# Order of the first stage of a transformer layer: projection weights, context tokens and the planner's price for 32-row products

## The chip, the cores and the metric

The kernel runs on one core of one Trainium2 chip. The metric is the device time of one execution in microseconds (us), given as the median of several runs. One execution has also been taken by the hardware profiler; all rows below come from that execution. A core has a matrix engine (TensorE, PE in the rows; its weight loads are PEld), a vector engine (DVE), a scalar engine (ACT), a general engine (GpSimd, POOL in the rows) and a queue engine that issues the transfers (SyncE, SP).

## The reference

The reference is one layer on 512 tokens of width 1024, with 256 context tokens beside them. Cut to what matters here:

```python
mod_lat = (silu(c) @ w_ada + b_ada); mod_ctx = (silu(c_ctx) @ w_ada + b_ada)
sa, sca, ga, sf, scf, gf = split(mod_lat, 6); csa, csca, ... = split(mod_ctx, 6)
h_lat = rmsnorm(x, attn_norm_w) * (1 + sca) + sa          # 512 x 1024
h_ctx = rmsnorm(ctx, attn_norm_w) * (1 + csca) + csa      # 256 x 1024
proj  = h @ w_in            # q, k, v of 4 differential heads, and low-rank q, kv of 4 MLA heads
...                         # rotary turn of q and k (latent tokens only), attention over 768 keys
x = x + ga * (mix @ w_out)
x = x + gf * moe(rmsnorm(x, ffn_norm_w) * (1 + scf) + sf) # 32 experts, top 4 of each token
out = rmsnorm(x, final_norm_w)
```

## The kernel before

The program first records every operation with its operands, and a **planner** (class `Plan`) then puts them in order. Each operation has a level; an engine takes, of the operations that could start first in the planner's own clock, the one with the lowest level. The planner's clock comes from `Plan.cost` (a duration for each operation) and from a model of the transfers as one bus. The order found is fixed: on the chip each engine runs its list in that order and waits where an operand is not there yet. Every recorded operation therefore has the same line, L282, in the profile, and is told apart by its tiles. Memory is planned as well: a tile can be placed only when an older tile of its ring has been used up, and, for names that are not in the `free` list of a store, only in the order of recording. A store can follow another one in the same memory: `att` and what stands on it (`rot`, with the rotary tables `trig` and the scratch tiles `rope1`, `rope2`) can be opened only when every operation on the store `start` has been placed and done. `start` holds the tokens `xt`, the modulation weights `wa`, and the scratch tiles `hv`.

The first stage goes like this:

- `load_wa(j)` brings the modulation weights of block j (2 MB, four transfers). Blocks 0, 2, 1 and 3 are loaded in this order, into 12 buffers for 16 transfers, so that block 3 waits for buffers of block 0.
- `modulation(j)` makes eight products of 32 rows (`sc<-wa,silp` in the rows), copies the sum out on ACT (`mrow<-sc`), brings it into columns with four small products (`oo<-pick,mrow`), and finishes `mod` and `gsc` on DVE. The tile `pa` that these small products write has the name `oo`.
- `normed` takes the root mean square of the tokens (squares on ACT, twelve tiny operations `rs_*` on DVE, then `xt<-xt,rs_y`).
- `modulated(k, which, ...)` turns 128 columns of the normed tokens (transposes `pj<-K,xt` and `tr<-K,xt`), applies scale and shift on ACT (`hv`), and splits the result into a high and a low part, `hTh` on DVE and `hTl` on DVE for the latent tokens (which = 0), on POOL for the context tokens (which = 1). The eight k of the latent tokens come in two groups of four; the second group needs block 3.
- `weights(src, n)` loads a chunk of projection weights in four transfers (`craw`, two buffers) and splits each into eight pairs `cwh` (ACT) and `cwl` (DVE).
- The projection loop takes chunk after chunk. The first chunk gives q and k of head 0: four tiles of 128 tokens, each with 8 x 3 products (`mm3`), in two banks named `pj` and two named `sc`. Each bank is read out by `rope`, which needs `trig` and writes on DVE and POOL (`rot`). Then come a product for the context tokens (`pj<-hTh,cwh`) and the next chunk, v, which wants the same four banks.
- Beside this, at level 3, run 64 transfers of further modulation weights (also shown as `wa`), scaled on ACT and summed on POOL (`ac<-ac,wa`).

After that the kernel has attention, output projection, routing, and 32 experts whose weights (`raw`, 12 MB each) are streamed.

Of the kernel before, what the change touches and what calls it, by code (L numbers as in the profile page):

```python
# [14 lines left out]
PSUM = bass.MemoryType.PSUM  # L15
DRAM = bass.MemoryType.DRAM

P = 128
NT = 4
# [181 lines left out]
class Plan:  # L201
# [22 lines left out]
    def cost(self, op, args):  # L224
        def cols(ap):
            n = 1
            for d in ap.shape[1:]:
                n *= d
            return n
        n = cols(args[0])  # L230
        if op.eng == "PE":
            if op.name == "transpose":
                return 0.107
            if args[2].dtype == F32:
                return 4 * max(n, 128) / 2400 / (2 if args[0].shape[0] == SMALL else 1)
            return max(n, 240) / 2400 * PEF / (2 if args[0].shape[0] == SMALL else 1)
        if op.eng == "ACT":
            extra = 0.1 if "accum_out" in op.kw or "bias" in op.kw else 0.0
            return 0.08 + extra + cols(args[1]) / 1200
        if op.eng == "POOL":  # L240
            return 0.06 + n / (1000 if op.name == "memset" else 247 if op.name.startswith(("tensor_scalar", "scalar_"))
                               else 420)
        n = max([cols(a) for a in args[:3] if hasattr(a, "shape")])
        fast = (op.name in ("tensor_copy", "tensor_scalar", "memset")
                and all(b.store.name not in ("ps", "mps") for b in op.bases))
        return 0.07 + n / (1850 if fast else 960)
# [85 lines left out]
def body(ctx, tc, x, ctxt, cc, w_ada, colw, b_arow, w_qk, w_v, w_m, w_uq, w_ukv, lams, w_out, ffn_w, router_w,  # L332
# [12 lines left out]
    const = store("const")  # L345
    small = store("small", const, free=("rs_m", "rs_i", "rs_y", "rs_t"))
    dram = store("dram", space=DRAM)
    ps = store("ps", free=("pj", "tr", "sc"), space=PSUM)
    start = store("start", small)
    att = store("att", small, (start,))  # L350
    rpl = store("rot", att)
# [128 lines left out]

    def modulated(k, which, t0, n):
        dst = slice(t0 * P, (t0 + n) * P)
        pt = bank(*(("pj", 2), ("pj", 2), ("tr", 1))[turn[0] % 3])
        turn[0] += 1
        for t in range(n):
            T.transpose(pt[:, t * P:(t + 1) * P], xt[t0 + t][:, k * P:(k + 1) * P], ident)
        hv = start.tile([P, n * P], F32, name="hv", bufs=3, padded_shape=[P, 512])
        S.activation(hv, pt[:, :n * P], AF.Identity, scale=gsc[:, k, which:which + 1], bias=mod[:, k, which:which + 1])
        V.tensor_copy(hTh[k][:, dst], hv)
        return (V if which == 0 else G).tensor_tensor(hTl[k][:, dst], hv, hTh[k][:, dst].bitcast(F32), op=OP.subtract)  # L490
# [20 lines left out]
    for k in range(4):  # L511
        modulated(k, 0, 0, NT)
    modulation(1)
    modulated_by = modulation(3)
    for k in range(4, KT):
        modulated(k, 0, 0, NT)


    plan.level = 4
# [2 lines left out]
    chunks = [qk_in[0], v_in[0], qk_in[1], qk_in[2], v_in[1], qk_in[3], (w_m[:, :, 0:256], 256, "cq", 0),  # L522
              (w_m[:, :, 256:448], 192, "ckv", 0)]

    def weights(src, n):
        for g in range(4):
            raw = pj.tile([P, 2, n], F32, name="craw", bufs=CRAW, padded_shape=[P, 2, 256])
            SP.dma_start(raw, src[:, 2 * g:2 * g + 2, :])
            for k in range(2):
                plan.side = 2.5  # L530
                a = pj.tile([P, n], F32R, name="cwh", bufs=CW, padded_shape=[P, 256])
                b = pj.tile([P, n], F32R, name="cwl", bufs=CW, padded_shape=[P, 256])
                split(raw[:, k, :], a, b)
                plan.side = EVAC
                yield a, b

    first = list(weights(*chunks[0][:2]))
    plan.level, plan.side = 0, None
    plan.level = 2.6
    for t in range(NCT):  # L540
        SP.dma_start(xt[NT + t], ctxt[t * P:(t + 1) * P, :])
    plan.level = 0
    normed(NT, NCT)
    for k in range(KT):
        ctx_ready = modulated(k, 1, NT, NCT)
# [42 lines left out]
    for ci, (src, n, kind, arg) in enumerate(chunks):  # L588
        cw = first if ci == 0 else list(weights(src, n))
        if kind == "v":  # L590
            heads["v", arg] = [att.tile([P, NKT, 256], F32R, name=n, bufs=2) for n in ("dvh", "dvl")]
        rot = []
        for t in range(NT if kind in ("cq", "qk") else NKT):
            ts = slice(t * P, (t + 1) * P)
            o = bank(*(("sc", 2) if ci < 2 and t % 2 else ("pj", 2)))
            for k, (a, b) in enumerate(cw):
                mm3(o[:, :n], hTh[k][:, ts], hTl[k][:, ts], a, b, k == 0, k == KT - 1,
                    **({"after": (modulated_by,)} if k == 0 else {}))
            if kind == "qk":
                rot.append(rpl.tile([P, 256], F32, name="rot", bufs=ROT))  # L600
                rope(o[:, 0:256], 4, t, rot[t])
            elif kind == "v":
                split(o[:, 0:256], *[v[:, t, :] for v in heads["v", arg]])
            elif kind == "cq":
                cq.append(rpl.tile([P, 256], F32, name="rot", bufs=ROT))
                S.copy(cq[t], o[:, 0:256])
                mj = rpl.tile([P, 256], F32, name="rope1", bufs=1)
                S.activation(mj, cq[t], AF.Square, scale=0.0625, accum_out=mss[:, 2 * t:2 * t + 1])
            else:
                ckv.append(rpl.tile([P, 192], F32, name="rot", bufs=ROT, padded_shape=[P, 256]))  # L610
                S.copy(ckv[t], o[:, 0:192])
                if t < NT:
                    rope(ckv[t][:, 128:192], 1, t, kr[:, t * 64:(t + 1) * 64])
                else:
                    G.tensor_copy(kr[:, t * 64:(t + 1) * 64], ckv[t][:, 128:192])
                mk = rpl.tile([P, P], F32, name="rope2", bufs=1, padded_shape=[P, 256])
                S.activation(mk, ckv[t][:, 0:128], AF.Square, scale=128.0 ** -0.5,
                             accum_out=mss[:, 2 * t + 1:2 * t + 2])
        if kind == "qk":
            kt = bank("pj", 2)  # L620
            for k, (a, b) in enumerate(cw):
                mm3(kt[:, :NCT * P], a[:, P:], b[:, P:], hTh[k][:, NT * P:], hTl[k][:, NT * P:], k == 0, k == KT - 1,
                    **({"after": (ctx_ready,)} if k == 0 else {}))
            A, B = ([att.tile([P, w], F32R, name=f"{name}{c}", bufs=2) for c in range(2)]
                    for name, w in (("dqs", NT * P), ("dks", KEYS)))
            Cl = att.tile([P, KEYS], F32R, name="dkl", bufs=2)
            qt = side_by_side([r[:, :P] for r in rot], A)
            for c, r in enumerate((LOW, HIGH)):
                stack_q(qt, r, DIFF_SCALE, A[c])
            main = side_by_side([r[:, P:] for r in rot], B + [Cl])  # L630
            for pt, d in ((main, slice(0, NT * P)), (kt, slice(NT * P, KEYS))):
                for c, r in enumerate((LOW, HIGH)):
                    stack_k(pt, r, d, B[c], Cl)
            heads[arg] = (A, B, Cl)
# [945 lines left out]
```

## Time and profile before

| what | us |
|---|---|
| median of 3 runs | 1553.77 |
| lowest and highest of them | 1551.37 and 1563.34 |
| the profiled execution, its own time | 1554.69 |
| its span, from the first to the last instruction | 1552.9 |

The span is what the rows cover; the profiled execution's own time is 1.8 us longer, and it lies 0.92 us above the median. TensorE was busy 1426.8 us of the span, DVE 975.9, ACT 820.8, POOL 627.2. A timeline row gives the start, the length, the engine, the operation with its tiles (written <- read), and in brackets how long the engine had been idle and what it waited for.

### The profile page before, as it was taken

To read this page: it belongs to the slowest core of one execution; us is meant where nothing else is said; L and a number is where in the kernel's file an instruction comes from. 1 tells how busy PE (TensorE), PEld (TensorE's weight loads), DVE (VectorE), ACT (ScalarE), POOL (GpSimd) and SP (SyncE) were. 2 spreads that over 40 slices of the span, in tenths; PEclk is the share of its full clock that TensorE was granted. 3 is DMA by queue.
4 is the path that set the end of the run, shared out by engine and by line. 5 is a ranking of instruction groups with operands and counts; after the bars stand their busy time and mean duration, and the time that the engine had idled before them with its cause. 6 is when DMAs were issued, how large, how long until landed. Compare 5 with 4: busy or idle time off the path is not lost.

```text
span 1552.9 us, 21067 instructions
## 1 busy us (share of the span) xinstructions
PE 1426.8 (92%) x7251; PEld 938.9 (60%) x7251; DVE 975.9 (63%) x1387; ACT 820.8 (53%) x1200; POOL 627.2 (40%) x544
## 2 busy tenths in 40 slices
PE   5798998998869999999999999999999999999993
PEld 2787887887646565464554646446364554636772
DVE  3878876776768666384563836547274562736995
ACT  3668866674537555263452635436263452635872
POOL 0553342002465354562735626364462734423111
PEclk9899999998969999999999999999999999999996
DMA  9433333007777999999999999999999999999944
GB/s 348 132 116 114 98 109 136 1 28 250 274 260 267 354 397 391 402 404 393 396 404 389 393 388 395 400 392 396 402 392 398 392 399 397 389 391 396 417 175 138
DMA packets 90895, 478.00 MB, mean 308 GB/s; under 512 B 12309, under 2 KB 14997, under 8 KB 42144
## 3 DMA queue, kind: packets, MB, share of 16 engines
q1 hardware_dynamic: 83040, 459.82, 75.9%
q0 software_dynamic: 7744, 16.79, 4.7%
q8 instruction: 58, 0.95, 0.2%
q14 instruction: 53, 0.43, 0.1%
HBM read 465.40 MB, written 18.24 MB: 311 GB/s over the span
## 4 chain that ended last, share of the span: by engine, by line
DMA 35%; PE 12%; issue 3%; DVE 2%; ACT 0%; SPq 0%; POOL 0%; DVEq 0%; POOLq 0%; ACTq 0%
DMA raw<-in_w 34%; PE gy L282 4%; PE gg L282 4%; PE gu L282 4%; DMA acc_d<-ys,si 1%; DVE wl L282 0%; PE tr L282 0%; DMA raw<-acc_d 0%; DVE raw L282 0%; ACT wh L282 0%; DVE fs L282 0%; ACT xh L282 0%; DVE act L282 0%; DVE rs_t L282 0%; POOL acc_d L1103 0%
## 5 line engine op out<-in xcount | busy, mean ns | idle before, releaser
L282 DVE TENSOR_TENSOR wl<-raw,wh 128x1024 fp32r<-128x1024 f32 x432 | 509.1, 1227 | 53.0 <-ACT wh L282 38.9
L282 ACT CAST wh<-raw 128x1024 fp32r<-128x1024 f32 x432 | 436.4, 1051 | 95.8 <-DMA raw<-in_w 31.1
L1103 POOL DMA_INDIRECT acc_d<-ys,si x17 | 123.2, 7245 | 219.4 <-DVE ys L282 219.4
L282 DVE TENSOR_SCALAR act<-gu 112x1024 f32<-112x1024 f32 (+1 forms) x32 | 31.7, 991 | 278.8 <-PE gu L282 278.8
L282 PE MATMUL gg<-raw,xh 128*64 128x512 f32 x448 | 163.0, 602 | 13.6 <-DMA raw<-in_w 13.6
L282 POOL TENSOR_SCALAR g<-g 112x1024 f32<-112x1024 f32 (+1 forms) x32 | 71.2, 2225 | 251.0 <-ACT g L282 251.0
L282 PE MATMUL gu<-raw,xh 128*64 128x512 f32 x448 | 160.9, 594 | 0.0
L282 ACT COPY g<-gg 112x1024 f32<-112x1024 f32 (+1 forms) x32 | 26.4, 825 | 248.4 <-PE gg L282 248.4
L282 POOL TENSOR_TENSOR ac<-ac,wa 128x512 f32<-128x512 f32 x56 | 77.0, 1376 | 123.8 <-ACT wa L282 110.7
L282 POOL TENSOR_SCALAR krhc<-K,krh 128x64 bf16<-128x64 f32 (+1 forms) x116 | 117.2, 1020 | 6.3 <-PE tr L282 6.3
L282 PE MATMUL gy<-raw,ah 128*64 128x512 f32 x448 | 116.7, 598 | 0.0
L282 PE MATMUL gg<-wh,xh 128*112 128x512 f32 x304 | 105.0, 407 | 2.6 <-ACT wh L282 1.5
L282 PE MATMUL gg<-wh,xl 128*112 128x512 f32 x304 | 99.9, 398 | 0.2 <-DVE xl L282 0.2
L282 PE MATMUL gg<-wl,xh 128*112 128x512 f32 x304 | 97.3, 397 | 1.1 <-DVE woraw L282 0.9
L282 PE MATMUL gy<-wh,ah 128*112 128x512 f32 x272 | 87.0, 400 | 12.1 <-ACT wh L282 12.1
L282 PE MATMUL gu<-wh,xl 128*112 128x512 f32 x288 | 95.1, 399 | 0.0
L282 PE MATMUL gu<-wh,xh 128*112 128x512 f32 x288 | 93.1, 396 | 0.0
L282 PE MATMUL gu<-wl,xh 128*112 128x512 f32 x288 | 92.1, 400 | 0.0
L282 PEld LDWEIGHTS gg<-raw,xh 128*64 128x64 f32 x448 | 42.9, 136 | 80.7 <-DMA raw<-in_w 41.6
L282 PE MATMUL gy<-wl,ah 128*112 128x512 f32 x272 | 88.0, 404 | 2.2
L282 PEld LDWEIGHTS gu<-raw,xh 128*64 128x64 f32 x448 | 47.5, 137 | 63.3 <-issue 62.6
L282 PE MATMUL gy<-wh,al 128*112 128x512 f32 x272 | 85.0, 394 | 0.0
(409 smaller groups left out, 2921.1 us busy)
## 6 DMA issues: line engine op xcount, KB each, us to landing
raw<-in_w SPq DMA_DIRECT2D x380, 1024.0 KB, 21.9
wa<-in_w_ada SPq DMA_DIRECT2D x64, 256.0 KB, 3.1
wa<-in_w_ada SPq DMA_DIRECT2D x16, 512.0 KB, 10.1
craw<-in_w_qk SPq DMA_DIRECT2D x16, 256.0 KB, 3.3
woraw<-in_w_out SPq DMA_DIRECT2D x8, 512.0 KB
raw<-in_w SPq DMA_DIRECT2D x8, 512.0 KB, 10.6
xt<-in_x SPq DMA_DIRECT2D x4, 512.0 KB
craw<-in_w_v SPq DMA_DIRECT2D x8, 256.0 KB, 3.7
```

Of the source, the lines that this page charges most:

```text
L282: getattr(self.engines[op.eng], op.name)(*args, **kw)
L1103: nc.gpsimd.indirect_dma_start(dst, bass.IndirectOffsetOnAxis(ap=si, axis=0), ys, None, bounds_check=halves * NT * P - 1, oob_is_err=False ...
```

## The change

Five edits, all in what the planner is given:

1. `Plan.cost` prices a product that writes 32 rows at a quarter instead of in full (64 rows stay at half).
2. The transfers and splits of the first chunk's weights get levels 0.1 and 0.2 (before: the first transfer 4, the splits 2.5; the later three transfers of the chunk keep 0.5).
3. The norm and `modulated` of the context tokens get level 0.3 instead of 0. The transfers of the context tokens keep 2.6.
4. `modulated` of the context tokens writes the one bank `oo` instead of the three `pj` and `tr`, and `oo` joins the `free` list.
5. The first product of each projection waits for the last transpose of the latent tokens (before: for the last product of modulation block 3), and for a tile of context tokens on the last `hTl` of the context tokens.

```diff
@@ class Plan, cost
             if args[2].dtype == F32:
-                return 4 * max(n, 128) / 2400 / (2 if args[0].shape[0] == SMALL else 1)
-            return max(n, 240) / 2400 * PEF / (2 if args[0].shape[0] == SMALL else 1)
+                return 4 * max(n, 128) / 2400 / {32: 4, 64: 2}.get(args[0].shape[0], 1)
+            return max(n, 240) / 2400 * PEF / {32: 4, 64: 2}.get(args[0].shape[0], 1)
@@ body
-    ps = store("ps", free=("pj", "tr", "sc"), space=PSUM)
+    ps = store("ps", free=("pj", "tr", "sc", "oo"), space=PSUM)
@@ modulated
-        pt = bank(*(("pj", 2), ("pj", 2), ("tr", 1))[turn[0] % 3])
+        pt = bank(*((("pj", 2), ("pj", 2), ("tr", 1)), (("oo", 1),))[which][turn[0] % (1 if which else 3)])
         turn[0] += 1
         for t in range(n):
-            T.transpose(pt[:, t * P:(t + 1) * P], xt[t0 + t][:, k * P:(k + 1) * P], ident)
+            modulated.moved = T.transpose(pt[:, t * P:(t + 1) * P], xt[t0 + t][:, k * P:(k + 1) * P], ident)
@@ after the second group of modulated
-    modulated_by = modulation(3)
+    modulation(3)
     for k in range(4, KT):
         modulated(k, 0, 0, NT)
+    modulated_by = modulated.moved
@@ weights
-    def weights(src, n):
+    def weights(src, n, low=2.5):
...
-                plan.side = 2.5
+                plan.side = low
...
-    first = list(weights(*chunks[0][:2]))
+    plan.level, plan.side = 0.1, 0.1
+    first = list(weights(*chunks[0][:2], 0.2))
     plan.level, plan.side = 0, None
     plan.level = 2.6
     for t in range(NCT):
         SP.dma_start(xt[NT + t], ctxt[t * P:(t + 1) * P, :])
-    plan.level = 0
+    plan.level = 0.3
     normed(NT, NCT)
@@ the projection loop
-                    **({"after": (modulated_by,)} if k == 0 else {}))
+                    **({"after": (modulated_by,) if t < NT else (ctx_ready,)} if k == 0 else {}))
```

## Rows read from the trace of the kernel before

**Rows 1.** The profile page: shares of the chain that ended last, by engine.

```profile
DMA 35%; PE 12%; issue 3%; DVE 2%; ACT 0%; SPq 0%; POOL 0%; DVEq 0%; POOLq 0%; ACTq 0%
```

**Rows 2.** Busy time by stretch (us: length, engines, PE clock, DMA share, GB/s).

```profile
0.00:47.20 47.20, 25.56 (x126) 11.22 (x126) 20.62 (x60) 18.74 (x33) 6.96 (x10) 0.84 0.83 305
...
80.00:360.00 280.00, 261.62 (x1878) 235.69 (x1879) 213.00 (x446) 204.37 (x411) 78.81 (x68) 0.97 0.28 88
...
828.00:1384.00 556.00, 532.58 (x2414) 290.98 (x2413) 291.75 (x277) 243.66 (x293) 258.62 (x205) 1.00 1.01 395
```

**Rows 3.** Timeline of the transfer queue SP, 10 to 36 us.

```profile
10.20 12.74 SPq L282 DMA_DIRECT2D wa<-in_w_ada  x12
...
34.09 2.95 SPq L282 DMA_DIRECT2D craw<-in_w_qk  x2
```

**Rows 4.** Timeline of PE, 32 to 57 us.

```profile
32.83 1.05 PE L282 MATMUL sc<-wa,silp 128*32 128x512 f32 x4 [0.23 <-DMA wa<-in_w_ada]
...
42.38 1.86 PE L282 MATMUL oo<-pick,mrow 128*128 128x2 f32 x8 [7.15 <-ACT mrow L282]
...
47.18 0.58 PE L282 MATMUL sc<-cwl,hTh 128*128 128x256 f32 x1 [2.40 <-DVE cwl L282]
...
55.81 0.44 PE L282 MATMUL pj<-K,xt 128*128 128x128 f32 x2 [0.53 <-ACT hv L282]
```

**Rows 5.** Timeline of ACT, 29 to 50 us.

```profile
29.64 0.59 ACT L282 COPY mrow<-sc 128x512 f32<-128x512 f32 x1 [0.52 <-PE sc L282]
...
41.75 0.58 ACT L282 COPY mrow<-sc 128x512 f32<-128x512 f32 x1
...
48.71 0.78 ACT L282 ACTIVATE hv<-pj,mod,gsc 128x512 f32<-128x512 f32 x1 [4.59 <-DVE gsc L282]
```

**Rows 6.** Timeline of DVE, 21 to 54 us.

```profile
21.07 2.74 DVE L282 TENSOR_SCALAR xt<-xt,rs_y 128x1024 f32<-128x1024 f32 x4
...
37.97 0.17 DVE L282 TENSOR_SCALAR rs_m<-ss 128x2 f32<-128x2 f32 x1 [6.42 <-ACT junk L282]
...
39.36 1.19 DVE L282 SCALAR_TENSOR_TENSOR rs_t<-rs_t,rs_m 128x2 f32<-128x2 f32 x1
...
43.28 3.51 DVE L282 TENSOR_SCALAR xt<-xt,rs_y 128x1024 f32<-128x1024 f32 x2
...
49.52 0.43 DVE L282 CAST hTh<-hv 128x512 fp32r<-128x512 f32 x1 [0.91 <-ACT hv L282]
...
53.13 0.69 DVE L282 TENSOR_TENSOR hTl<-hv,hTh 128x512 fp32r<-128x512 f32 x1
```

**Rows 7.** Timeline of POOL, 39 to 47 us.

```profile
39.26 6.98 POOL L282 TENSOR_TENSOR ac<-ac,wa 128x512 f32<-128x512 f32 x5 [38.42 <-ACT wa L282]
```

**Rows 8.** Instructions on tile hv, 20 to 64 us (ns min/median/max, first to last start).

```profile
L282 ACT ACTIVATE hv<-tr,mod,gsc x5: 562/566/777, 27.6 to 59.4; 128x256 f32<-128x256 f32 x3, 128x512 f32<-128x512 f32 x2
L282 POOL TENSOR_TENSOR hTl<-hv,hTh x8: 780/802/918, 56.2 to 62.0; 128x256 fp32r<-128x256 f32 x8
```

**Rows 9.** Timeline of POOL, SP, DVE and PE, 61 to 81 us.

```profile
61.97 0.85 POOL L282 TENSOR_TENSOR hTl<-hv,hTh 128x256 fp32r<-128x256 f32 x1 [0.23 <-DVE hTh L282]
...
62.85 0.33 SPq L282 DMA_DIRECT2D trig<-in_cst  x1
...
66.93 0.80 DVE L282 TENSOR_TENSOR rope<-pj,trig 128x256 f32<-128x256 f32 x3
...
67.88 0.36 PE L282 MATMUL pj<-hTh,cwh 128*128 128x256 f32 x1 [1.79 <-DVE rope L282]
...
80.82 0.36 PE L282 MATMUL pj<-cwh,hTh 128*128 128x256 f32 x1 [1.60 <-DVE dqs L282]
```

**Rows 10.** Busy time by stretch again, in short windows (columns as in the second group).

```profile
38.00:40.00 2.00, 0.00 (x0) 0.00 (x0) 1.76 (x8) 2.00 (x4) 0.74 (x1) 0.72 0.58 195
48.00:52.00 4.00, 4.00 (x21) 4.00 (x20) 2.99 (x10) 3.04 (x5) 0.00 (x0) 0.50 0.65 196
52.00:54.00 2.00, 2.00 (x17) 1.92 (x15) 2.00 (x5) 2.00 (x7) 0.00 (x0) 0.87 0.01 3
```

## The prediction

> **What bounds the kernel now.** I began with the chain that ended last [rows 1]: transfers hold 35% of it. It starts deep in the expert phase and says nothing of the first 400 us, but it tells how a gain there travels: from 828 to 1384 us the weights stream at 395 GB/s with the DMA engines full [rows 2], so whatever starts that stream earlier ends the kernel earlier by the same amount. Between 80 and 360 us TensorE is busy 261.6 of 280 us [rows 2]; there, too, an earlier start is passed on, and at most 18.4 us of holes could be won or lost. The loose stretch is the first: 25.6 busy us in 47.2 [rows 2].
>
> Second view, the timelines of the first 70 us. The last data of modulation block 3 let TensorE run at 32.83, and its products are over at 33.88 [rows 4]. The copy `mrow` that continues this starts only at 41.75 [rows 5]; ACT's list had other work in front of it, since the planner priced the eight products four times too long. TensorE waits 7.15 us for it [rows 4], the second group of `modulated` starts at 48.71 [rows 5], and the first projection at 47.18 with its first four k [rows 4].
>
> Third view, what the projection runs into. Its four banks are emptied by `rope`, which needs `trig`; the queue issues `trig` at 62.85, just after the last `hTl` of the context tokens ends at 61.97 + 0.85 = 62.82 [rows 9]. That is the store `start` becoming free. `rope` starts 4.1 us after that end, at 66.93, and TensorE, idle for 1.79 us, goes on at 67.88 [rows 9]. So two chains end together here: the four q tiles, and the context tokens. **Call the end of the last context `hTl` C; before, C is 62.82.** The change hurries the first chain and lowers the second.
>
> **The change part by part.** *Weights ahead of block 3.* All twelve transfers after the tokens leave the queue in one row of 12.74 us, the weights of the first chunk only at 34.09 [rows 3]. With level 0.1 and 0.5 two of them (0.52 MB) get in where block 3 waits for buffers; at 395 GB/s [rows 2] that delays block 3 by 1.3 us, from 32.83 to 34.1. The other two wait in the queue for the first splits, and the context tokens stand behind them: another 1.3 us. Their statistics were ready at 37.97 [rows 6]; 2.6 us later is 40.6, still before DVE is free for them (below), so this costs nothing; without that cover it would cost those 2.6 us.
>
> *Price of a quarter.* Products end at 34.1 + 1.05 = 35.2, `mrow` (0.59 [rows 5]) at 35.8, the small products at 36.9 (I take half of the 1.86 us that they took at the half clock, [rows 4], and a hand-off). Three DVE operations of 0.2 each (the seven from 37.97 to 39.36 come 0.2 us apart [rows 6]) bring `hv` of k = 4 to about 37.7, **11.0 us earlier** than 48.71. The four k then took DVE from 49.52 to 53.82 [rows 6], with ACT's first `hv` 5.1 us in all; one weight split in between makes 4.7 without it. So DVE is through with the latent tokens at 42.4, or 43.6 if ACT is first sent to a square of the context tokens (two squares had to be over before 37.97; I price one at 1.2 us).
>
> *New wait of the projections.* The last transposes need the bank that the first `hv` empties at 38.5; two of them take 0.44 us [rows 4], four 0.9, so q can start at 39.4, **7.8 us earlier** than 47.18. Queued behind that wait on TensorE are only projections, which before began on the first four k; they lose nothing. The 96 products of q then have some 20 us before anybody can empty their banks.
>
> *Context tokens lower, on one bank.* This decides. The twelve `rs_*` operations and the two `xt` now come behind the latent tokens. Alone they would take 12 x 0.2 = 2.4 us, and 2 x 0.69 = 1.4 (four took 2.74 [rows 6]): 46.2. Beside POOL's sums from 39.26 to 46.24 [rows 7] they took 43.28 - 37.97 = 5.3 and 3.5 us, one operation 1.19 instead of 0.16 to 0.17 [rows 6]: 43.6 + 8.8 = 52.4. Before, they ended at 46.79. Then come eight k on one bank: `hv` 0.56 [rows 8] and transposes 0.44 [rows 4] can no longer overlap, with two hand-offs of 0.1 that makes 1.2 us a k, 9.6 for eight; behind the last there are a cast (0.3) and POOL's `hTl` 0.80 [rows 8] with their hand-offs, 1.3. So C lies between 46.2 + 10.9 = 57.1 and 52.4 + 10.9 = 63.3, **5.7 us earlier to 0.5 later** than 62.82. POOL's sums will be there again, since their weights come right behind the context tokens, but only three of them before their four buffers are to be filled anew; nearest to that is the middle, C = 60.2: **-2.6 us**.
>
> How does DVE lose to POOL? In the trace as blocking: a two-column operation grows by about a whole microsecond while sums of 1.3 us run. The Trainium skill (SBUF — State Buffer, section "Who interferes with whom") says that a DVE operation with two SBUF inputs and a POOL operation that reads SBUF share a port pair as a lock, and that the loser waits for the whole instruction. Row and rule agree; by the rule alone, with sums all along, this stretch would come out at its late end.
>
> *TensorE at the restart.* At half clock 21 instructions took 4 us [rows 10], so the 96 of q take some 9 us at full clock and with waits for the last k perhaps 12; q is over at 49 to 52, and `rope` comes at 60.2 + 4.1 = 64.3. In between TensorE has eight times 0.44 us to do. Before, an idle TensorE was at 0.72 of its clock by 38 to 40 us and at 0.50 when the projection had started, through 48 to 52 [rows 10]. Four such microseconds do the work of two, so the restart loses 2.0 us; the hole of 1.60 us before 80.82, where TensorE waits for DVE [rows 9], takes up most. I take **+0.4**, ends 0 and 2.0.
>
> *Bank `oo` free in order.* In attention the order of `oo` is also that of the transposes, and in the routing one bank still serves one user after another; nothing is gained by name alone, and I price it at 0. What hides it is that order. But a new plan may also move work elsewhere, in both directions; of the 18.4 us of holes I allow a third, 6 us, to each side.
>
> Sum: -2.6 + 0.4 = **-2.2 us**. The profiled execution's 1554.69 becomes 1552.5; it lies 0.92 above the median, so the median becomes **1551.6**.
>
> **The rivals.** *Everything is carried.* If the projection's earlier start came through, -7.8, and its products, which ran at half clock from 47.18 to about 52.5 [rows 10], ran at full clock, -2.6, the time would be 1553.8 - 10.4 = 1543.4. For it speaks the full TensorE from 80 us on. Against it: C would have to come at 52.4, and even without POOL the sum above gives 57.1.
>
> *The context tokens come last.* Slower: if POOL's sums run through the whole norm, C is 63.3; one sum of 1.3 us set before the last `hTl` makes it 64.6, 1.8 late, and the cold restart counts in full with 2.0: 1553.8 + 3.8 = 1557.6. It decides as soon as the context `xt` end after 51.9. For it: five sums stood in that very stretch before. Against it: the four buffers.
>
> *The plan behind changes more than the front.* The first 80 us come out as forecast, and a hole opens or closes in attention or routing: 1551.6 less or plus 6 us, 1545.6 or 1557.6.
>
> *It does not do what it says.* Block 3's copy still stands behind transfers on ACT's list; then the front stays as it is, 1553.8.
>
> **How the numbers follow.** Forecast 0.45, carried in full 0.13, context last 0.20, plan behind 0.16 (half to each side), no effect 0.06. A measurement of this kernel tells about 1% (15.5 us) from no change, since its three runs lie 12 us apart. None of the cases reaches that alone; for the carried start with a closed hole (1537.4), and for the context tokens last with holes opened twice over (1569.6), I give 0.08 and 0.07, and 0.85 for within 1%. The range goes from the carried start, 1543.4, to the slow cases, 1557.6, and at both ends a little further (1.4 and 2.4 us) for the halves of those cases that lie beyond their mark: 1542 to 1560.
>
> **What would show it.** In the profile of the changed kernel: `mrow` within 1 us of block 3's last product, at 35 to 36 us; the first projection at 39 to 41; two weight transfers ahead of block 3's; the last context `hTl` ending between 57 and 63 with `trig` right behind it; a TensorE that is mostly idle from about 52 to 64 us and restarts at half clock. I am wrong if `rope` starts before 58 us (then the carried case holds), if the context norm is over before 45 us, or if the stretch from 80 to 360 us has grown or shrunk by more than 6 us.

## The result, and the profile after

The changed kernel takes 1572.38 us (median of 20 runs, 1566.51 to 1576.67); the kernel before, beside it on the same chip, 1555.32 us (20 runs, 1551.21 to 1565.35). The ratio is 1.0097, 95% interval [1.0084, 1.0111]: **slower by about 15 us**, on the other side of the forecast and outside its range. The ratio is not the quotient of the medians: these are 17.1 us apart, while 1.0097 stands for 15.1. The profiled executions have spans of 1572.2 and 1552.9 us, so the two traces differ by 19.3 us, 2 us more than the medians and 4 more than the ratio says.

First the chain that ended last, the row that answers to [rows 1]:

```profile
DMA 27%; PE 20%; DVE 3%; issue 1%; ACT 1%; DVEq 0%; SPq 0%; ACTq 0%
```

TensorE has 20% of it instead of 12%, transfers 27% instead of 35%. The page names the TensorE part: it is products of the experts (`gg`, `gy`, `gu`), so this row, too, says nothing of the first 400 us. Then busy time by stretch, as in [rows 2], with a stretch around the restart of TensorE added:

```profile
80.00:360.00 280.00, 256.45 (x1802) 230.76 (x1801) 211.19 (x432) 194.56 (x397) 81.21 (x71) 0.95 0.25 80
828.00:1384.00 556.00, 533.97 (x2415) 297.29 (x2415) 302.34 (x285) 251.68 (x301) 270.15 (x210) 1.00 1.01 394
60.00:80.00 20.00, 11.86 (x64) 9.18 (x64) 10.13 (x25) 9.15 (x19) 12.14 (x15) 0.66 0.37 119
```

The same added stretch of the kernel before:

```profile
60.00:80.00 20.00, 16.91 (x133) 15.71 (x131) 16.96 (x33) 11.41 (x27) 11.72 (x13) 1.00 0.54 170
```

The expert stream is what it was, 394 against 395 GB/s: next to nothing is lost there, and nothing given back. From 80 to 360 us TensorE does 1802 instructions where it did 1878, in 5.2 us less busy time and at a mean granted clock of 0.95 instead of 0.97 [rows 2]. From 60 to 80 us it does 64 where it did 133.

A direct way to see where the time goes is to count TensorE's products in the order of their starts and to compare when the n-th one starts. This table is worked out from the traces in that way (us later than before; a trace may lack a few records). A third trace tells how far such distances can be trusted: the control replay_before, described below, has the order of the kernel before, and its products start 0.5 to 2.0 us later than before at the first five of these counts, and 1.5 us earlier at the 2600th.

| product | start before | changed | later by |
|---|---|---|---|
| 300 | 75.5 | 80.6 | 5.1 |
| 600 | 118.4 | 126.1 | 7.8 |
| 900 | 165.0 | 178.0 | 13.0 |
| 1600 | 264.6 | 275.1 | 10.5 |
| 2000 | 327.2 | 345.3 | 18.1 |
| 2600 | 469.3 | 486.8 | 17.5 |
| 6200 | 1281.0 | 1300.4 | 19.4 |

So a first part of the loss, 5 us, is there when the projections get going; a larger part comes **between 118 and 327 us**, in attention; behind that the distance only stays. Of the five edits only the fourth reaches into that stretch by itself: `oo`, now in the `free` list, is also the bank of attention's value products (`oo<-pth,dvh`).

**The front.** SP's timeline, the answer to [rows 3]:

```profile
10.12 7.87 SPq L282 DMA_DIRECT2D wa<-in_w_ada  x8
18.94 1.60 SPq L282 DMA_DIRECT2D craw<-in_w_qk  x2
21.56 4.15 SPq L282 DMA_DIRECT2D wa<-in_w_ada  x4
34.91 1.00 SPq L282 DMA_DIRECT2D craw<-in_w_qk  x2
35.95 0.90 SPq L282 DMA_DIRECT2D xt<-in_ctxt  x2
```

Two weight transfers go ahead of block 3, two wait until the first splits have emptied `craw`. Block 3's products on PE:

```profile
34.27 1.92 PE L282 MATMUL sc<-wa,silp 128*32 128x512 f32 x16
```

They end at 36.2 and had not waited for data. What the held-back transfers do is seen on ACT, the answer to [rows 5]:

```profile
36.26 0.59 ACT L282 COPY mrow<-sc 128x512 f32<-128x512 f32 x1 [1.81 <-PE sc L282]
37.96 0.71 ACT L282 CAST cwh<-craw 128x256 fp32r<-128x256 f32 x2 [1.11 <-DMA craw<-in_w_qk]
39.93 0.71 ACT L282 CAST cwh<-craw 128x256 fp32r<-128x256 f32 x2 [1.26 <-DMA craw<-in_w_qk]
41.34 1.06 ACT L282 ACTIVATE junk<-xt 128x1024 f32<-128x1024 f32 x1 [0.70 <-DMA xt<-in_ctxt]
...
42.39 0.76 ACT L282 ACTIVATE hv<-pj,mod,gsc 128x512 f32<-128x512 f32 x1
```

`mrow` is early, at 36.26. But ACT's list then has two pairs of splits and a square, each waiting for a transfer that was issued at 34.91 or later, and only then `hv` of k = 4 (`gsc`, its last operand, was over at 41.48; the square then held ACT until 42.4). DVE, in its timeline, has the same in its list:

```profile
38.40 0.76 DVE L282 TENSOR_TENSOR cwl<-craw,cwh 128x256 fp32r<-128x256 f32 x2 [2.85 <-ACT cwh L282]
40.36 0.42 DVE L282 TENSOR_TENSOR cwl<-craw,cwh 128x256 fp32r<-128x256 f32 x1 [1.21 <-ACT cwh L282]
40.71 0.16 DVE L282 TENSOR_TENSOR mod<-oo,cols 128x8 f32<-128x8 f32 x1
...
46.57 0.16 DVE L282 TENSOR_SCALAR rs_m<-ss 128x2 f32<-128x2 f32 x1
...
48.79 1.27 DVE L282 SCALAR_TENSOR_TENSOR rs_t<-rs_t,rs_m 128x2 f32<-128x2 f32 x1
...
54.42 1.42 DVE L282 TENSOR_SCALAR xt<-xt,rs_y 128x1024 f32<-128x1024 f32 x2
```

`mod`, which `hv` needs, stands at 40.71 behind them. The context norm starts at 46.57 and ends at 55.84 (before: 46.79). Behind it, POOL:

```profile
48.72 5.45 POOL L282 TENSOR_TENSOR ac<-ac,wa 128x512 f32<-128x512 f32 x4 [47.88 <-ACT wa L282]
...
64.76 1.37 POOL L282 TENSOR_TENSOR ac<-ac,wa 128x512 f32<-128x512 f32 x1
66.09 0.72 POOL L282 TENSOR_TENSOR hTl<-hv,hTh 128x256 fp32r<-128x256 f32 x1
67.05 1.10 POOL L282 TENSOR_TENSOR hTl<-hv,hTh 128x256 fp32r<-128x256 f32 x1 [0.23 <-DVE hTh L282]
```

Meanwhile TensorE has little to do (4.6 us busy between 59 and 72, before 10.9), and its clock falls. The transposes of the context tokens on PE, and one of the stretches in which they run:

```profile
60.78 0.44 PE L282 MATMUL oo<-K,xt 128*128 128x128 f32 x2 [0.71 <-ACT hv L282]
61.93 0.69 PE L282 MATMUL oo<-K,xt 128*128 128x128 f32 x2 [0.72 <-ACT hv L282]
```

```profile
62.00:64.00 2.00, 1.28 (x4) 0.51 (x4) 1.27 (x2) 0.56 (x1) 1.85 (x3) 0.50 0.00 0
```

The last cast on DVE, beside the seventh `hTl`:

```profile
66.12 0.84 DVE L282 CAST hTh<-hv 128x256 fp32r<-128x256 f32 x1 [1.11 <-ACT hv L282]
```

The gate, on SP, DVE and PE, the answer to [rows 9]:

```profile
68.18 0.33 SPq L282 DMA_DIRECT2D trig<-in_cst  x1
70.81 0.82 DVE L282 TENSOR_TENSOR rope<-pj,trig 128x256 f32<-128x256 f32 x3 [1.89 <-DMA trig<-in_cst]
71.69 0.58 PE L282 MATMUL pj<-hTh,cwh 128*128 128x256 f32 x1 [3.48 <-DVE rope L282]
```

C is 67.05 + 1.10 = 68.15 us, **5.3 us later** than before. `trig` follows at once, as forecast, and `rope` 2.7 us after C, where the forecast took 4.1 from the kernel before.

**The order behind.** One hole stands for several. TensorE waits for `dqs` ahead of the first score product of a head in both kernels. The changed kernel, on PE, and the stretches behind that wait:

```profile
165.25 0.38 PE L282 MATMUL sc<-dks,dqs 128*128 128x256 f32 x1 [2.35 <-DVE dqs L282]
```

```profile
166.00:168.00 2.00, 1.91 (x13) 1.73 (x13) 1.91 (x5) 1.99 (x5) 0.00 (x0) 0.87 0.79 265
...
170.00:172.00 2.00, 2.00 (x6) 1.12 (x6) 1.75 (x4) 0.97 (x3) 0.00 (x0) 0.50 0.10 39
...
176.00:178.00 2.00, 2.00 (x12) 2.00 (x11) 2.00 (x4) 1.79 (x4) 1.92 (x2) 0.57 0.08 19
```

The same wait of the kernel before, and what is behind it:

```profile
154.83 0.47 PE L282 MATMUL sc<-dks,dqs 128*128 128x256 f32 x1 [1.91 <-DVE dqs L282]
```

```profile
154.00:156.00 2.00, 0.92 (x3) 0.68 (x4) 1.91 (x4) 1.96 (x5) 0.00 (x0) 0.73 0.89 278
156.00:158.00 2.00, 2.00 (x11) 2.00 (x10) 1.97 (x8) 1.86 (x5) 0.00 (x0) 0.50 0.15 53
158.00:160.00 2.00, 2.00 (x16) 1.76 (x14) 0.69 (x2) 1.24 (x4) 0.00 (x0) 0.92 0.52 172
```

A wait of about the same length is followed by some 3 us at half clock (1.2 GHz) in one kernel and by some 10 in the other. It is not an accident of one execution that the clock falls there: the control replay_before has the same wait, on PE, and the same fall in the stretches behind it:

```profile
156.24 0.36 PE L401 MATMUL sc<-dks,dqs 128*128 128x256 f32 x1 [1.90 <-DVE dqs L401]
```

```profile
156.00:158.00 2.00, 1.39 (x7) 1.25 (x7) 1.88 (x5) 1.88 (x5) 0.00 (x0) 0.78 0.58 201
158.00:160.00 2.00, 2.00 (x12) 2.00 (x11) 1.69 (x8) 1.65 (x4) 0.00 (x0) 0.50 0.18 57
```

Stretches of 2 us from 80 to 360 us, summed, give the whole: idle 18.4 us before and 23.5 after; busy time lost to the clock (busy times one minus granted clock) 7.2 and 14.6. So in the same 280 us the changed kernel does 5.1 + 7.4 = 12.5 us less work at full clock. The second part is the less certain one: in the five traces that have the order of before in this stretch (the control and three mixed kernels beside the kernel before) the loss to the clock is 4.5 to 10.0 us, and the changed order was traced once.

The single runs say how much of the slowdown goes with the clock at all, since each has its mean granted clock on record. Of the 85 runs of the kernel before that stand beside the experiments, those at 0.961 took 1556.7 to 1564.8 us, those at 0.960 1558.4 to 1560.0; the changed kernel at 0.961 took 1566.5 to 1569.0, at 0.960 1569.8 to 1572.0. At equal clock it is still some 9 to 11 us longer. So the larger part of the loss does not go with the mean clock; this is a comparison of runs, not an experiment.

### The profile page after: what moved, and what is told of

Same layout as the page of the kernel before. It is cut to its first block, busy times and chain, and to the rows that moved or that the text cites. A ratio compares the mean times of both kernels' runs of the same rounds, so it can differ in the third digit from the quotient of the medians.

```text
span 1572.2 us, 21079 instructions
## 1 busy us (share of the span) xinstructions
PE 1435.9 (91%) x7251; PEld 945.4 (60%) x7251; DVE 980.0 (62%) x1387; ACT 822.4 (52%) x1200; POOL 633.0 (40%) x544
## 4 chain that ended last, share of the span: by engine, by line
DMA 27%; PE 20%; DVE 3%; issue 1%; ACT 1%; DVEq 0%; SPq 0%; ACTq 0%
DMA raw<-in_w 27%; PE gg L282 7%; PE gy L282 7%; PE gu L282 6%; DVE wl L282 2%; PE tr L282 1%; ACT wh L282 1%; DMA raw<-acc_d 0%; DVE raw L282 0%; ACT xh L282 0%; DVE act L282 0%; DVE fs L282 0%; DVE rs_t L282 0%; DVE woraw L282 0%; DVE ys L282 0%
```

## The experiments

Two questions were put. Does the loss come from the front (**theory B**: what the edits do there stays to the end), or does a part of it come from the new order that the planner made for everything behind (**theory A**)? And what is the loss behind made of?

To tell front from order, some kernels plan as they would and from a point on follow the order of another kernel, written out as a list of recorded operations:

```diff
+        rank = {n: i for i, n in enumerate(listed())}
+        ends = {e: sorted((o for o in self.ops if o.eng == e), key=lambda o: rank[o.order[1]]) for e in avail}
...
+                if cut:
+                    for op in [o for o in ends[e] if o not in gone][:AHEAD]:
+                        t = self.place(op) if op in index else None
...
+            if not cut and start >= CUT:
+                cut = True
```

All ratios are to the kernel before, run beside each kernel on the same chip.

| run | median us | before | ratio [95%] |
|---|---|---|---|
| replay_before | 1555.30 | 1556.83 | 0.9990 [0.9973, 1.0008] |
| front_after_rest_before | 1559.43 | 1556.83 | 1.0014 [0.9996, 1.0032] |
| ctx_first_rest_before | 1557.35 | 1556.83 | 1.0004 [0.9983, 1.0025] |
| weights_late | 1573.64 | 1556.83 | 1.0110 [1.0068, 1.0151] |
| after_until_120us | 1563.11 | 1556.42 | 1.0050 [1.0030, 1.0071] |
| after_until_195us | 1570.32 | 1556.42 | 1.0074 [1.0038, 1.0109] |
| old_price | 1571.35 | 1556.42 | 1.0110 [1.0077, 1.0142] |
| neutral_replan | 1562.42 | 1556.42 | 1.0044 [1.0025, 1.0063] |
| after_holes_filled | 1570.64 | 1553.85 | 1.0096 [1.0063, 1.0129] |
| before_holes_filled | 1552.88 | 1553.85 | 0.9984 [0.9963, 1.0005] |
| mended_front_rest_before | 1560.38 | 1553.85 | 1.0037 [1.0014, 1.0059] |
| after_holes_filled_short | 1570.34 | 1555.79 | 1.0088 [1.0065, 1.0110] |
| before_holes_filled_short | 1550.52 | 1555.79 | 0.9966 [0.9951, 0.9982] |
| neutral_replan_2 | 1553.00 | 1555.79 | 0.9982 [0.9966, 0.9998] |

**The order of before as a list (replay_before).** `CUT = 0` on the kernel before: a control.

> The kernel before, with the planner's order written out as a list and followed from the first operation on (control for the two runs with mixed orders). Both theories expect the time before: ratio 0.998 to 1.002.

Ratio 0.9990: a written list costs nothing by itself that can be measured, so the next runs can be read.

**Front of the changed kernel, rest as before (front_after_rest_before).** The changed kernel up to the first projections, then the order of before.

> The changed kernel up to the first rotary operation (61 us of the planner's clock), and behind it the kernel before's order on every engine, written out as a list. Theory A, the order behind: the changed front costs 4 to 5 us (the first rope came 3.9 us later, the 300th product 5.1 us), and the other 12 to 14 us come from the new order that the planner found between 80 and 380 us; so this kernel stands 4 to 6 us above before, 1559 to 1561. Theory B, the front alone: a late front breaks the interplay behind it whatever the order; then this kernel stands 13 to 17 us above before, 1568 to 1572.

Its last `hTl` on POOL ends late, though 1.4 us earlier than in the changed kernel:

```profile
64.79 2.00 POOL L401 TENSOR_TENSOR hTl<-hv,hTh 128x256 fp32r<-128x256 f32 x2
```

C is 66.79, `rope` starts at 69.5, and the 300th product is 4.8 us later than before. Yet the median is only 2.6 us above before. Theory B, which needed 13 or more, falls: all five edits are in force in this kernel's front, and it does not lose what the changed kernel loses.

**Context tokens first, rest as before (ctx_first_rest_before).** The changed kernel's front with the context transfers ahead, then the order of before.

```diff
-    plan.level = 2.6
+    plan.level = 0.05
     for t in range(NCT):
         SP.dma_start(xt[NT + t], ctxt[t * P:(t + 1) * P, :])
```

> The changed kernel with the transfers of the context tokens moved ahead of the first chunk's weights and of modulation block 3 (level 0.05 instead of 2.6), and behind the first rotary operation the kernel before's order. Theory A with the last context hTl as the gate: in the planner's clock that hTl ends at 54.5 instead of 58.4 (changed) and 55.1 (before), and the rest is the old order; on the chip the context norm falls into DVE's free time before block 3, so rope should start at 60 to 64 us and the kernel stand 2 to 6 us below before, 1549 to 1553. Theory B: the q projection matters, which here starts about as in the changed kernel; then the same as the run with the changed front, within 1 us.

C came at 62.1, `rope` at 64.8, 2.1 us earlier than before, and the time did not follow (ratio 1.0004): a miss. By the 300th product this kernel is not ahead of before either (1.3 us later in the trace), so an earlier gate by itself was not passed on.

**The changed kernel without edit 2 (weights_late).**

```diff
-    plan.level, plan.side = 0.1, 0.1
-    first = list(weights(*chunks[0][:2], 0.2))
+    first = list(weights(*chunks[0][:2]))
```

> The changed kernel without its second edit: the first chunk's weights at their old levels 4, 0.5 and 2.5. In the changed kernel ACT's and DVE's lists wait at 37 to 41 us for the third and fourth weight transfer, in front of the second group of modulated. Theory A: that wait goes, the second group starts by 38 to 39 instead of 42.4 us, the last context hTl ends 3 to 5 us earlier than 68.2; but the order behind is new again, so the total can lie anywhere from 5 below to 15 above before. Theory B: as the front is mended, so is the total: 0 to 5 us above before.

Without the weight transfers in ACT's list, `hv` comes behind `mrow` and two squares of the context tokens; ACT and POOL:

```profile
35.64 0.59 ACT L282 COPY mrow<-sc 128x512 f32<-128x512 f32 x1 [3.03 <-PE sc L282]
36.12 1.06 ACT L282 ACTIVATE junk<-xt 128x1024 f32<-128x1024 f32 x1
...
37.30 1.06 ACT L282 ACTIVATE junk<-xt 128x1024 f32<-128x1024 f32 x1
...
38.35 0.76 ACT L282 ACTIVATE hv<-pj,mod,gsc 128x512 f32<-128x512 f32 x1
```

```profile
63.16 1.86 POOL L282 TENSOR_TENSOR hTl<-hv,hTh 128x256 fp32r<-128x256 f32 x2 [0.56 <-DVE hTh L282]
```

`hv` is 4.0 us and C, at 65.02, 3.1 us earlier than in the changed kernel. The total is as slow as with edit 2 (1.0110). So the front was mended in part and the order behind was not: product 300 is 3.1 us later than before, product 2000 17.0 us.

**That front, rest as before (mended_front_rest_before).**

> The changed kernel without edit 2 (weights of the first chunk not ahead of block 3) up to the start of the projections' second tile, then the order of before as a written list. Theory A (front and order behind add up): the front of the run without edit 2 ended its last context hTl at 65.0, 2.2 us later than before and 3 us earlier than the changed kernel; 0 to 3 us above before, below the changed front with the order of before (1559.4). Theory B (the edits' front costs what the changed kernel lost): 13 us or more above before.

With the order of before, it comes down from 1.0110 to 1.0037; theory A holds in its main part. The size is a miss: 6.5 us above before, not 0 to 3, and not below the changed front with the order of before (the intervals overlap). The two fronts cost 2.2 and 5.8 us by the ratios, with intervals from -0.6 to 9.2 us; which of the two is the dearer isn't shown, nor what within them costs it.

**Changed order up to 118 us, and up to 195 us (after_until_120us, after_until_195us).** The same switch, later.

> The changed order of all engines up to TensorE's 582nd operation (about 118 us on the chip), then the order of before as a written list. Theory A (the loss is spread over the order behind the front, in several holes and stretches of low clock): only what the changed kernel had lost by then can remain, 7.8 us at 118 us, of which the expert stream takes a part back, as it did with the front alone: 3 to 7 us above before. Theory C (the loss sits in one place, the hole of 3.9 us and the half clock near 280 us): the same as with the front alone, 2 to 4 us above before. Theory B (whatever the front delays stays to the end, and the rest follows from it): 13 us or more above.

> The changed order of all engines up to TensorE's 1163rd operation (about 195 us on the chip), then the order of before as a written list. Theory A (spread): the changed kernel was 10.8 us late there; 6 to 11 us above before, clearly more than with the cut at 118 us. Theory C (one place near 280 us, which this kernel doesn't have): 2 to 5 us above before, like the cut at 118 us. Theory B: 13 us or more.

By the ratios, the loss grows with the point of the switch: front alone 0.14%, up to 118 us 0.50%, up to 195 us 0.74%, all 0.97%. Theory C, a single place near 280 us, would have left the first two cuts alike with the front; the cut at 195 us already carries about 11.5 of 15 us. The steps one by one are as large as their intervals, so only the growth is shown, not the share of each stretch. In the trace of the cut at 118 us the distance stays at 7.4 to 8.3 us from product 1000 on, where the order of before has taken over.

**The changed kernel without edit 1 (old_price).**

```diff
-                return 4 * max(n, 128) / 2400 / {32: 4, 64: 2}.get(args[0].shape[0], 1)
-            return max(n, 240) / 2400 * PEF / {32: 4, 64: 2}.get(args[0].shape[0], 1)
+                return 4 * max(n, 128) / 2400 / (2 if args[0].shape[0] == SMALL else 1)
+            return max(n, 240) / 2400 * PEF / (2 if args[0].shape[0] == SMALL else 1)
```

> The changed kernel without edit 1: products into 32 rows priced in full again, the other four edits kept. Theory P (the price is what spoils the order behind; the other edits only move the front): the order behind is as good as before's, 0 to 5 us above before. Theory A (any new order behind the front comes out with its own holes, and none is better planned than another): a third order, not the one of before; 8 to 25 us above before, with mrow of block 3 behind transfers again at 40 us or later.

Slower by 15 us (medians) or 17 (ratio) as well. Block 3's `mrow` is back at its old place (41.75), the 300th product is 2.0 us later than before, hardly more than in the control, and this kernel loses its time elsewhere: 11 us between its products 1600 and 1700. The other four edits are enough for a loss of this size; the price is not needed for it.

**The kernel before, planned again with a constant changed by little (neutral_replan, neutral_replan_2).** `LAG = 2.1` for 2.0; `BUS = 361e3` for 360e3.

> The kernel before with one constant of the planner's clock changed (the transfers' lag 2.0 to 2.1 us), none of the five edits. Front within 1 us of before (last context hTl at 62 to 64). Theory A (the order behind is as good as luck made it, and before's is a well chosen one): another order, 3 to 15 us slower than before. The rival (only the edits hurt, a re-plan by itself costs nothing): within 2 us of before.

> The kernel before with another constant of the planner's clock changed (the bus from 360 to 361 bytes per ns), none of the five edits. Front within 1 us of before. Theory A (each new order brings a time of its own; the first neutral re-plan came out 6.0 us slower): a shift of 2 to 12 us, most likely to the slow side. Its rival (the first was an accident): within 2 us of before.

The first came out 6.0 us slower, the second 2.8 us faster, both outside no change by their intervals (the second barely: its upper end is 0.9998), with the front where it was (at the 300th product 0.5 us from before in the first; the last `hTl` ends at 63.04 in the second). So re-planning alone moves this kernel by several us, and to either side. That before's order is an especially good one, as theory A had put it, is not borne out: the second order is at least as good.

**TensorE's holes filled (four runs).** Throw-away products, put into TensorE's list by `Plan.emit` ahead of instructions that were seen to wait there for data; the planner does not know of them, so the order stays as it is.

```diff
+        for _ in range(FILL.get(key + (self.seen[key],), 0)):
+            if kw.get("start", True):
+                self.nc.tensor.matmul(args[0][:, 0:P], k, k, start=True, stop=True)
+            else:
+                self.nc.tensor.matmul(args[0][:, 0:64], k[0:64, :], k[0:64, 64:P], start=False, stop=False)
```

> The changed kernel in its own order, with throw-away products put into TensorE's list just ahead of eight instructions that were seen to wait there for data (64 products, up to the length of the hole each: the score products that wait for dqs, value products that wait for pth or ptl, and others between 113 and 319 us). They read the unit matrix and write a bank that is free at that point, or add zero. Theory K (the half clock that follows such holes is a loss of its own, 7.4 of the 12.7 us of work lost from 80 to 360 us, and it goes when TensorE is not left idle): 3 to 8 us below the changed kernel, so 1564 to 1569, with a mean granted clock above 0.97 from 80 to 360 us. Rival theory H (only the idle time counts; the clock drops wherever it will): within 2 us of the changed kernel or slower, clock at 0.95 as before.

> The kernel before in its own order, filled in the same way at nine places (55 throw-away products, 101 to 272 us). It had 7.2 us of work lost to the clock from 80 to 360 us. Theory K: 2 to 6 us faster than before, clock 0.98 or more in that stretch. Theory H: within 2 us of before.

Both came out within 2 us of their unfilled kernels. These two were not clean: the filling ran past the longest holes, as on PE in the kernel before, filled (the hole had 2.19 us):

```profile
261.51 3.74 PE L277 MATMUL oo<-K 128*128 128x128 f32 x32
```

So a second pair with fewer products, which end inside their holes:

> As after_holes_filled, with 43 throw-away products, so few at each of the eight places that they end inside the hole (in the earlier run those ahead of the longest hole, 3.86 us, took about 7 us and ran past it). Theory K (the half clock behind the holes is a loss of its own): 3 us or more below the changed kernel, so 1569 or less, and a ratio to before below 1.0080. Theory H (only the idle time and what ends it count): within 2 us of the changed kernel.

> As before_holes_filled, with 41 throw-away products that end inside their holes (earlier those of the two holes at 260 and 263 us took 6.4 us instead of 3.8). Theory K: 2 to 5 us faster than before, clock 0.98 or more from 80 to 360 us. Theory H: within 1.5 us of before.

In the kernel before, theory K holds: 5.3 us faster, ratio 0.9966. The wait for `dqs` that was shown above looks like this now, on PE and in the stretches behind:

```profile
154.00 1.72 PE L277 MATMUL sc<-K 128*128 128x128 f32 x14
...
156.08 0.35 PE L299 MATMUL sc<-dks,dqs 128*128 128x256 f32 x1 [0.35 <-DVE dqs L299]
```

```profile
80.00:360.00 280.00, 270.06 (x1971) 243.79 (x1972) 212.19 (x446) 205.22 (x412) 79.40 (x68) 0.99 0.28 88
...
154.00:156.00 2.00, 1.73 (x15) 1.53 (x14) 1.80 (x4) 1.91 (x4) 0.00 (x0) 1.00 0.71 207
156.00:158.00 2.00, 1.50 (x9) 1.16 (x9) 1.91 (x5) 1.99 (x5) 0.00 (x0) 1.00 0.57 189
```

The score product still waits for DVE, and the clock stays at 2.4 GHz (1.00 where it was 0.73 and 0.50). The first filled run of this kernel has 1.00 there as well, so two traces without products in the wait show the fall and two with them do not. The gain goes with the clock: the mean over the ten runs is 0.971, against 0.964 in the unfilled runs beside them. In the changed kernel the same filling did not do it; the windows of that run:

```profile
80.00:360.00 280.00, 264.43 (x1904) 238.81 (x1902) 211.94 (x436) 196.60 (x400) 82.05 (x71) 0.96 0.25 80
...
160.00:180.00 20.00, 17.76 (x114) 15.50 (x113) 16.45 (x38) 14.85 (x33) 4.26 (x4) 0.83 0.27 91
...
280.00:300.00 20.00, 17.80 (x98) 14.79 (x98) 14.24 (x37) 7.16 (x14) 2.95 (x4) 0.83 0.21 85
```

The ratio went from 1.0097 to 1.0088, and two low stretches stayed. The first filling had lifted the clock of this kernel further (6.5 us of busy time lost to it from 80 to 360 us, against 14.6 unfilled) and also won nothing that can be measured. The four runs of that first filling have a mean clock of 0.965, about that of the kernel before, and a median of 1570.64 us. So for the changed kernel theory K is not shown: a clock as in the kernel before did not bring it back to that kernel's time. How its loss of some 13 us behind the front divides into waits, clock and, in these runs, the throw-away products themselves stays open. The filled kernel before is the fastest of the study.

## Why the prediction was wrong

**What held.** `mrow` at 36.26, right behind its products (forecast 35.8); two weight transfers ahead of block 3; `trig` right behind C; a mostly idle TensorE, if from 59 to 72 us instead of 52 to 64, and its restart at half clock (0.66 from 60 to 80 us); losses carried almost unchanged through the expert stream (17.5 us at product 2600, 19.4 at 6200). That block 3's products came near the forecast time does not confirm the 1.3 us priced for its transfers: they ran as one row from 34.27 to 36.2, behind other work of PE and without a wait for data. The rival "context tokens come last" was the right one for the front: it decides "as soon as the context `xt` end after 51.9", and they ended at 55.84; its price, 3.8 us, lies near the 2.6 that the front alone cost.

**The gate, forecast 60.2, measured 68.15.** The miss of 8.0 us has three terms. First, "`hv` of k = 4 to about 37.7" came at 42.39. The step that failed is the sentence that the late context transfers wait behind a cover, "so this costs nothing": I asked what the two held-back weight transfers delay in SP's queue, and not where their splits stand in the lists of ACT and DVE, ahead of `mod` and `hv`. Without edit 2 `hv` came at 38.35, with two squares and no split ahead of it on ACT, so the sum up to `hv` was good to 0.7 us; the splits are what it lacked (for one square it had allowed, in the later of its two ends). Through this q began at 43.97 instead of 39.4, and the context norm began at 46.57, 3.6 us behind the middle of 42.4 and 43.6. Second, the norm took 9.3 us against 3.8 to 8.8, because four sums of POOL ran beside it, not three, and splits of weights stood between its operations; the middle was the wrong point to choose: 3.0 us. Beside the sums every second two-column operation took 1.15 to 1.27 us and the one behind it 0.16, as without sums, in the manner of [rows 6]; this agrees again with the Trainium skill (SBUF — State Buffer, "Who interferes with whom"), by which the loser of the shared port pair waits for a whole instruction of the other. Third, eight k on one bank with their tail took 12.3 us against 10.9: 1.4 us. About half of it is TensorE's clock, which the forecast counted only behind the gate: it fell while the engine was mostly idle, and the last three pairs of transposes ran at 0.50 and took 0.69 us each instead of 0.44. The rest is the tail, 2.1 us against 1.3: a sum of POOL at 64.76 held back the seventh `hTl`, and beside that one the last cast took 0.84 us instead of 0.3; the last `hTl` itself took 1.10 instead of 0.80.

**What the gate is worth.** Forecast -2.2, and by the measured gate it would have been about +5: the 300th product is 5.1 us late. But the front alone, run to the end with the order of before, cost 2.6 us by the medians (-0.6 to 5.0 by the interval), and the mended front 6.5 (2.2 to 9.2). That the gate is passed on to the end one to one is therefore not shown; the front with the earliest gate gained nothing.

**The order behind, forecast "a third, 6 us, to each side".** This term was mis-sized, and it is the larger part of the miss. Each kernel less its own front with the order of before, by the ratios: 15.1 - 2.2 = 12.9 us for the changed kernel, 17.1 - 5.8 = 11.3 without edit 2. In the sum the term stood at nothing, and its bound was a share of the 18.4 us of holes that were there. Two things were left out: a new order can make *new* holes (23.5 us idle), and busy time counts at the granted clock (14.6 us of it lost instead of 7.2, with the spread between executions that was given above). The neutral re-plans, +6.0 and -2.8 us, say that 6 us was a fair size for an order that is planned again after a small change; the three plans that have the edits, with or without the price and the early weights, are all 15 to 17 us slower. Why these orders are worse than the neutral ones is open. Shown is that neither the price nor the early weights are needed for it. Edits 3, 4 and 5 were not taken back one at a time; the fourth, which frees the order of `oo` in attention as well and which the forecast priced at nothing, is a rival that no run tests.

**The chances.** Each piece was among the rivals, with 0.20 and 0.16; both together, and on the slow side, were named only as a tail of 0.07 at 1569.6. They are not independent: the changed front is itself what makes the planner plan anew, so the two belong in one case.

## What to carry to other kernels

When a planner orders the work, an edit at the front is also a re-plan of everything behind; price that by planning again with a neutral change and timing it, not by a share of the holes that can be seen. Here even that would have given some 6 us, against the 11 to 13 that the edited plans lost; only the old order, written out as a list behind the new front, told the two apart. When work is hurried on one queue, look where its *consumers* stand in the in-order lists of the other engines: a transfer that is late by itself holds up what is listed behind its first reader. A wait of TensorE costs more than its length where the clock drops behind it, and filling such waits with throw-away products paid 5 us in the kernel before; in the changed kernel it paid nothing that can be measured.

## What the runs showed of the hardware

TensorE ran at half clock behind waits of only about 2 us: after 1.91 us idle with a further 0.25 the granted clock was 0.73 and then 0.50 (before, 154 to 158 us), and after 2.35 us it stayed near 0.50 for some 10 us (changed kernel). With products put into the first of these waits it was 1.00 throughout, and with nine such waits filled the kernel was 0.34% faster although TensorE had 41 products more to do. Where the half clock falls differs between executions of one order: the control lost 9.3 us of busy time to it from 80 to 360 us, the kernel before 7.2. Within one kernel the time goes largely with the clock: the second neutral re-plan had a mean granted clock of 0.971 in a run of 1550.96 us and 0.961 in one of 1562.63 us.

An idle TensorE also slowed the chain it was waiting for: at a granted clock of 0.50 a pair of transposes took 0.69 us instead of 0.44, and each stood between two `hv` of ACT (changed kernel, 61.93 us on). DVE was held up beside POOL: every second two-column operation took 1.15 to 1.27 us instead of 0.16 beside sums of about 1.36 (changed kernel, 48.7 to 54.2 us).
